# Order of the elements in the PSUM eviction of the gate products (hybrid decoder step, 1 core)

## The chip, the cores and the metric

The kernel runs on one core of one Trainium2 chip. The time is device microseconds of one execution; before the change the median of 3 runs is 2963.49 us (2955.86 to 2965.84).

## The reference, cut to what matters

One inference step of two layers for 512 prompt tokens and 8 sample tokens. Each layer is a token mixer, a layer norm, a PEER block and another layer norm. The change lies in the PEER block. Per token it picks 8 heads x 16 experts out of 16384 and adds up their contributions:

```python
expert = jnp.take_along_axis(cand_idx, pos, axis=-1)
gate = jax.nn.softmax(best, axis=-1)
act = jax.nn.gelu(jnp.einsum('td,thkd->thk', tb, u_tab[expert]).astype(F32))
return jnp.einsum('thk,thkd->td', (gate * act).astype(tb.dtype), v_tab[expert])
```

## The kernel before, in words

The first 384 prompt tokens (three token tiles of 128) are computed densely, over all 16384 experts. An expert has the number i*128 + j; the 128 experts with the same i form a block, and j is the partition. For each block, `u_step` (line 354) multiplies the block's weights with the 384 tokens in 24 matmuls (`pu`, lines 91 to 93: f16 high and low halves) and ScalarE applies the gelu into `act` (line 366). The weights of a block come by DMA into `wst`; ScalarE rounds them to `wh` (line 77) and VectorE makes the rest `wl` (line 86). `wh` and `wl` have two buffers each, and `wst` three. The other 128 prompt tokens and the 8 sample tokens use gathered rows instead (`gather`, line 387; `g_dot`, line 394).

For the dense tokens the kernel needs the gate of every (expert, token) pair, which is zero except for the 128 chosen experts of a token. `gates` (line 514) makes them for 32 tokens at a time, 12 calls per layer. For 8 tokens VectorE builds four one-hot arrays `oh` (lines 530 to 533); TensorE multiplies them per token, two 128x128 matmuls each (lines 537 and 538), into one PSUM bank `pg` that holds four tokens as [token][i]; there are four such banks. ScalarE then copies `pg` into `stage` (line 540, by the helper of line 77), an SBUF tile of [i][32 tokens] per partition j. After eight such copies `stage` goes to DRAM (`GD`, line 544), 2 MB on the queue of ScalarE. `stage` has one buffer, so the first copy of a call waits until the transfer of the call before has landed.

The calls of `u_step` stand between the calls of `gates`: two before the copies of a call and one in its middle (lines 518 and 543). Between the groups of four calls stands the top-k work for the next token tile (`pairs`, line 488, on VectorE). A scheduler fixes the order on each engine at build time; each engine then runs its own queue in that order.

After the gates follows the main phase: `gl<-GD` loads the gates back, VectorE multiplies them with `act` (line 640), and TensorE multiplies the product with the value rows (`yps`, line 654), with the remaining `u_step` calls between. Its buffers `yac`, `row` and others lie where `stage` lay.

Of the kernel before, what the change touches and what calls it, by code (L numbers as in the profile page):

```python
# [70 lines left out]
class Kern:  # L71
# [249 lines left out]
    def peer(self, layer):  # L321
# [51 lines left out]
        def run_u(k):  # L373
            for _ in range(k):
                u_step()
# [99 lines left out]
        with tc.tile_pool(name="gates", bufs=1, reuse_waits="tile") as gp, \  # L475
# [38 lines left out]
            def gates(t, part, us):  # L514

                lt = lts[t]
                stage = gp.tile([P, P, TG], F32, name="stage")
                run_u(us - 1)
                order = self.last_on(S)
                for t4 in range(0, TG, 4):  # L520
                    if t4 % 8 == 0:

                        sl = slice(part * TG + t4, part * TG + t4 + 8)

                        def tok(k):
                            return lt[:, k, sl].rearrange("p (a b) -> p a b", b=2)[:, :, None, :].to_broadcast([P, 4, P, 2])

                        io = self.iota2[:, None].to_broadcast([P, 4, P, 2])
                        oh = gp.tile([P, 4, 4, P, 2], F16, name="oh", bufs=2)
                        V.tensor_tensor(oh[:, 0], io, tok(1), op=OP.is_equal)  # L530
                        V.tensor_tensor(oh[:, 1], io, tok(0), op=OP.is_equal)
                        V.tensor_mul(oh[:, 2], oh[:, 1], tok(2))
                        V.tensor_mul(oh[:, 3], oh[:, 1], tok(3))
                    pg = psum.tile([P, 4, P], F32, name="pg", bufs=4)
                    for k in range(4):
                        q, r = divmod(t4 % 8 + k, 2)
                        T.matmul(pg[:, k], oh[:, 0, q, :, r], oh[:, 2, q, :, r], start=True, stop=False)
                        T.matmul(pg[:, k], oh[:, 0, q, :, r], oh[:, 3, q, :, r], start=False, stop=True)  # L538
                    with self.behind(order):
                        self.copy(stage[:, :, t4:t4 + 4].rearrange("p i t -> p t i"), pg)  # L540
                    order = []
                    if t4 == TG // 2:
                        run_u(1)
                nc.scalar.dma_start(GD[P // TG * t + part], stage)
# [20 lines left out]
            for k in range(12):  # L565
                gates(k // 4, k % 4, self.UG)
                acc[0] += self.GU
                while acc[0] >= 1:
                    g_ustep()
                    acc[0] -= 1  # L570
                if k % 4 == 3 and k < 11:
                    run_u(self.UP)
                    pairs(k // 4 + 1)
                    pairs_t(k // 4 + 1)
# [1176 lines left out]
```

## Time and profile before

| what | value |
|---|---|
| median of 3 runs | 2963.49 us |
| time of the profiled execution | 2954.78 us |
| its span | 2953.1 us |
| granted TensorE clock, mean | 0.989 |
| TensorE busy (PE) | 2824.2 us, 96% |
| VectorE busy (DVE) | 2501.0 us, 85% |
| ScalarE busy (ACT) | 1351.7 us, 46% |
| GpSimd busy (POOL) | 956.7 us, 32% |
| copies `stage<-pg` | 192, 182.7 us in sum |

The 192 copies lie in two stretches, from 598.8 us on in the first layer and up to 2215.3 us in the second. PE stands for matmuls, PEld for the loads of their weights; DVE, ACT and POOL are VectorE, ScalarE and GpSimd. A row of a view gives a line of the program, the engine, the operation, the tile written and the tiles read, and the shape as partitions x elements. Busy shares are averages over stages with different limits, and a matmul's row lasts longer than the step from one matmul to the next.

### The profile page before, as it was taken

The numbers are of one execution on the slowest core, as the hardware profiler recorded it, in microseconds if no ns is written. First come the engines' busy times: TensorE is split into PE (matmuls) and PEld (weight loads), VectorE is DVE, ScalarE is ACT, GpSimd is POOL, SyncE is SP. The second block draws the span as 40 slices with busy tenths as digits, with TensorE's granted clock in tenths as the row PEclk, the third lists the DMA queues.
The fourth block names the chain that finished last, engine by engine and source line by source line (L and its number), as shares of the span: only waits on it lengthen the run. The fifth ranks groups of instructions, "written<-read, shape, count | busy, mean of one in ns | idle before, by whom it ended". The sixth has DMA issues, their size and how long they took to land.

```text
span 2953.1 us, 49153 instructions
## 1 busy us (share of the span) xinstructions
PE 2824.2 (96%) x18198; PEld 1714.9 (58%) x18198; DVE 2501.0 (85%) x5483; ACT 1351.7 (46%) x2127; POOL 956.7 (32%) x702
## 2 busy tenths in 40 slices
PE   8999999899999999999998999989999999999998
PEld 7787686466655555544447658646665555554443
DVE  6755789999878898889985869999988889888998
ACT  4733473266743333333435747236674333333332
POOL 2300151310034554445530014140005455444652
PEclk9999999999999999999999999999999999999999
DMA  4223495975699999999984348686569999999996
GB/s 134 71 83 129 147 330 193 311 253 199 225 380 357 372 362 369 360 324 375 354 289 162 106 144 299 238 296 223 211 252 382 355 374 363 355 347 346 330 368 223
DMA packets 320324, 811.33 MB, mean 275 GB/s; under 512 B 28099, under 2 KB 150411, under 8 KB 316244
## 3 DMA queue, kind: packets, MB, share of 16 engines
q1 hardware_dynamic: 229228, 455.37, 44.7%
q0 software_dynamic: 78336, 285.25, 26.0%
q10 hardware_dynamic: 12520, 67.58, 6.2%
q8 instruction: 142, 2.33, 0.3%
q14 instruction: 98, 0.80, 0.1%
HBM read 707.25 MB, written 99.46 MB: 273 GB/s over the span
## 4 chain that ended last, share of the span: by engine, by line
PE 59%; DMA 13%; DVE 12%; ACT 7%; issue 6%; POOL 3%; ACTq 0%; SPq 0%; POOLq 0%; DVEq 0%
PE yps L654 24%; PE pu L93 7%; PE pu L91 7%; PE pu L92 7%; DMA row<-in_u_rows,elist 3%; DMA gl<-GD 3%; ACT stage L77 2%; POOL row L390 2%; DMA gst<-in_uT 1%; DVE row L397 1%; ACT wh L77 1%; DVE wl L86 1%; PE psg L1034 1%; DMA row<-in_v_rows 1%; PE pg L538 1%
## 5 line engine op out<-in xcount | busy, mean ns | idle before, releaser
L654 PE MATMUL yps<-vv,vw 128*128 128x512 f16 x4536 | 1008.4, 380 | 10.4 <-DVE vv L86 8.4
L654 PEld LDWEIGHTS <-vw 128*128 128x128 f16 x4608 | 450.7, 98 | 546.1 <-issue 19.6
L390 POOL DMA_INDIRECT row<-in_v_rows,elist x272 | 398.1, 1463 | 836.3 <-ACT stage L77 425.0
L93 PE MATMUL pu<-xh,wl 128*128 128x384 f16 x1728 | 565.8, 329 | 28.5 <-DVE wl L86 28.1
L91 PE MATMUL pu<-xh,wh 128*128 128x384 f16 x1728 | 567.5, 328 | 21.7 <-ACT wh L77 21.7
L92 PE MATMUL pu<-xl,wh 128*128 128x384 f16 x1728 | 566.9, 328 | 0.0
L390 POOL DMA_INDIRECT row<-in_u_rows,elist x272 | 385.8, 1418 | 509.5 <-DVE yac L592 129.3
L86 DVE SCALAR_TENSOR_TENSOR wl<-wst,wh 128x1024 f16<-128x1024 f32 x284 | 351.3, 1240 | 165.8 <-ACT wh L77 151.7
L77 ACT ACTIVATE wh<-wst 128x1024 f16<-128x1024 f32 x284 | 299.3, 1054 | 403.5 <-PE pu L92 293.3
L77 ACT ACTIVATE vv<-row 128x1024 f16<-128x1024 f32 x252 | 264.2, 1051 | 369.6 <-PE yps L654 291.7
L91 PEld LDWEIGHTS <-wh 128*128 128x128 f16 x2816 | 279.9, 99 | 166.3 <-ACT wh L77 39.1
L93 PEld LDWEIGHTS <-wl 128*128 128x128 f16 x2816 | 277.5, 99 | 168.5 <-DVE wl L86 38.5
L86 DVE SCALAR_TENSOR_TENSOR vv<-row,vv 128x1024 f16<-128x1024 f32 x252 | 307.7, 1222 | 63.6 <-ACT vv L77 60.2
L92 PEld LDWEIGHTS <-wh 128*128 128x128 f16 x2816 | 277.7, 99 | 132.8 <-issue 5.9
L592 DVE SCALAR_TENSOR_TENSOR yac<-row,wgt,yac 128x1024 f32<-128x1024 f32 x268 | 343.3, 1281 | 8.7 <-DMA row<-in_v_rows,elist 6.7
L397 DVE CUSTOM_DVE_ANT_0 row<-row,xtok 128x1024 f32<-128x1024 f32 x256 | 308.4, 1220 | 20.7 <-DMA row<-in_u_rows,elist 20.5
L77 ACT ACTIVATE vw<-act 128x384 f16<-128x384 f32 x256 | 129.3, 514 | 226.8 <-PE yps L654 191.5
L77 ACT ACTIVATE stage<-pg 128x512 f32<-128x512 f32 x192 | 182.7, 1104 | 71.1 <-DMA GD<-stage 42.9
L366 ACT ACTIVATE act<-pu 128x384 f32<-128x384 f32 x256 | 121.7, 477 | 87.0 <-PE pu L93 86.1
L84 DVE TENSOR_TENSOR vw<-act,vw 128x384 f16<-128x384 f32 x256 | 139.3, 553 | 13.8 <-ACT vw L77 13.4
L640 DVE TENSOR_TENSOR act<-act,gl 128x384 f32<-128x384 f32 x256 | 127.6, 552 | 11.2 <-DMA gl<-GD 9.1
L92 PE MATMUL pq<-xl,wh 128*128 128x264 f16 (+1 forms) x480 | 132.9, 277 | 0.7 <-DVE xl L84 0.7
(502 smaller groups left out, 4138.8 us busy)
## 6 DMA issues: line engine op xcount, KB each, us to landing
row<-in_v_rows SPq DMA_DIRECT2D x256, 512.0 KB
wst<-in_uT SPq DMA_DIRECT2D x216, 512.0 KB
GD<-stage ACTq DMA_DIRECT2D x24, 2048.0 KB
gl<-GD SPq DMA_DIRECT2D x64, 768.0 KB
gst<-in_uT SPq DMA_DIRECT2D x40, 512.0 KB
PW<-gpr SPq DMA_DIRECT2D x40, 512.0 KB
wpr<-PW SPq DMA_DIRECT2D x40, 512.0 KB
wst<-in_wq SPq DMA_DIRECT2D x32, 512.0 KB
```

Of the source, the lines that this page charges most:

```text
L77: self.nc.scalar.activation(out, in_, AF.Copy, scale=scale)
L84: eng.tensor_sub(lo, src, hi)
L86: eng.scalar_tensor_tensor(lo, src, scale, hi, op0=OP.mult, op1=OP.subtract)
L91: mm(out, wh, xh, start=start, stop=False)
L92: mm(out, wh, xl, start=False, stop=False)
L93: mm(out, wl, xh, start=False, stop=stop)
L366: S.activation(t, ps[:, 0:ND], AF.Gelu_apprx_tanh, scale=1.0 / SCW)
L390: G.indirect_dma_start(out=r, out_offset=None, in_=src, in_offset=bass.IndirectOffsetOnAxis(ap=elist[:, k:k + 1], axis=0))
L397: V.tensor_tensor_reduce(u, u, self.xtok[:, 0] if k < P else xrep, 1.0, 0.0, OP.mult, OP.add, hd[:, k:k + 1])
L592: V.scalar_tensor_tensor(dst, vbuf.pop(n), wgt[:, k:k + 1], dst, op0=OP.mult, op1=OP.add)
L640: V.tensor_mul(a6, a6, gl)
L654: T.matmul(yps[t][:, o], w[:, a, c], v[:, b, o], start=x == 0 and k == 0, stop=x == P - 1 and k == 2)
```

## The change

One line. The copy of a PSUM bank of four tokens into `stage` walks through both tiles in another order. Before, it read `pg` from end to end, and wrote each token's 128 values into `stage` with a step of 32 elements (128 bytes). After, it writes for each i four tokens in a row (16 bytes; the next four elements are 128 bytes on), and reads `pg` with a step of 128 elements (512 bytes), four times, then goes on to the next i. What is computed, the number of instructions, and the order on every engine stay the same.

```diff
                     with self.behind(order):
-                        self.copy(stage[:, :, t4:t4 + 4].rearrange("p i t -> p t i"), pg)
+                        self.copy(stage[:, :, t4:t4 + 4], pg.rearrange("p t i -> p i t"))
                     order = []
```

## Rows read from the trace of the kernel before

**Rows 1.** Page, part 1 (busy time) and part 4 (chain, by line).
```profile
PE 2824.2 (96%) x18198; PEld 1714.9 (58%) x18198; DVE 2501.0 (85%) x5483; ACT 1351.7 (46%) x2127; POOL 956.7 (32%) x702
...
PE yps L654 24%; PE pu L93 7%; PE pu L91 7%; PE pu L92 7%; DMA row<-in_u_rows,elist 3%; DMA gl<-GD 3%; ACT stage L77 2%; POOL row L390 2%; DMA gst<-in_uT 1%; DVE row L397 1%; ACT wh L77 1%; DVE wl L86 1%; PE psg L1034 1%; DMA row<-in_v_rows 1%; PE pg L538 1%
```

**Rows 2.** Busy time by stretch, first layer: start:end, length, busy (instructions), granted clock, DMA.
```profile
core 0: us, PE busy (x) PEld busy (x) DVE busy (x) ACT busy (x) POOL busy (x), PEclk, DMA share, GB/s
598.00:690.00 92.00, 86.52 (x688) 56.82 (x686) 88.79 (x219) 61.74 (x78) 5.34 (x4) 1.00 0.66 231
690.00:828.00 138.00, 135.91 (x1165) 92.86 (x1163) 118.88 (x170) 96.67 (x120) 3.40 (x3) 1.00 0.65 235
```

**Rows 3.** ACT, groups by line and form: count | busy us, mean ns | idle before.
```profile
L77 ACT ACTIVATE stage<-pg 128x512 f32<-128x512 f32 x192 | 182.7, 1104 | 71.1 <-DMA GD<-stage 42.9 <-PE pu L92 24.0 <-PE pg L538 4.1
...
L77 ACT ACTIVATE scs<-psc 128x512 f32<-128x512 f32 x32 | 19.0, 595 | 9.0 <-issue 8.3 <-PE psc L445 0.7
...
L77 ACT ACTIVATE ss<-psc 128x8 f32<-128x8 f32 x32 | 5.8, 182 | 0.0
...
L77 ACT ACTIVATE xh<-pst 64x64 f16<-64x64 f32 x2 | 0.4, 218 | 2.0 <-PE pst L1546 2.0
```

**Rows 4.** Waits of PE, 598 to 690 us: us in total, times, longest.
```profile
PE pu L91 <- ACT wh L77: 3.5, 2, 2.1
PE pu L93 <- DVE wl L86: 2.0, 3, 1.1
```

**Rows 5.** Waits of DVE, 598 to 690 us.
```profile
DVE wl L86 <- ACT wh L77: 2.3, 2, 1.9
DVE lt L510 <- ACT lt L77: 0.5, 1, 0.5
```

**Rows 6.** Waits of PE, 690 to 828 us.
```profile
PE pu L91 <- ACT wh L77: 1.3, 4, 0.4
PE pu L93 <- DVE wl L86: 0.8, 1, 0.8
```

**Rows 7.** ACT in order of time, 750 to 778 us: start, length, instruction, idle before.
```profile
752.00 3.73 ACT L77 ACTIVATE stage<-pg 128x512 f32<-128x512 f32 x4 [3.69 <-DMA GD<-stage]
...
756.86 3.77 ACT L77 ACTIVATE stage<-pg 128x512 f32<-128x512 f32 x4
760.65 0.33 ACTq L544 DMA_DIRECT2D GD<-stage  x1
...
767.85 3.77 ACT L77 ACTIVATE stage<-pg 128x512 f32<-128x512 f32 x4 [3.98 <-DMA GD<-stage]
```

**Rows 8.** PE in order of time, 776.9 to 778.6 us.
```profile
777.26 0.33 PE L92 MATMUL pu<-xl,wh 128*128 128x384 f16 x1
777.42 0.33 PE L93 MATMUL pu<-xh,wl 128*128 128x384 f16 x1
...
778.11 0.34 PE L91 MATMUL pu<-xh,wh 128*128 128x384 f16 x1 [0.24 <-ACT wh L77]
...
778.50 0.22 PE L537 MATMUL pg<-oh 128*128 128x128 f16 x1
778.56 0.22 PE L538 MATMUL pg<-oh 128*128 128x128 f16 x1
```

**Rows 9.** Waits of PE, second layer, 1998 to 2082 us.
```profile
PE pu L91 <- ACT wh L77: 3.6, 3, 1.8
PE pu L93 <- DVE wl L86: 2.4, 3, 1.1
```

**Rows 10.** Waits of DVE, second layer, 1998 to 2082 us.
```profile
DVE wl L86 <- ACT wh L77: 2.9, 1, 2.9
```

**Rows 11.** Waits of PE, second layer, 2082 to 2220 us.
```profile
PE pu L91 <- ACT wh L77: 1.1, 3, 0.4
```

**Rows 12.** DVE in order of time, just after the last copy of the first layer.
```profile
835.33 0.75 DVE L590 TENSOR_SCALAR yac<-row,wgt 128x1024 f32<-128x1024 f32 x1 [2.42 <-DMA GD<-stage]
```

## The prediction

> **What bounds the kernel now.** I read the page first, then the stretches with the gate copies, then who waits for whom in them. TensorE is busy 96% of the span, ScalarE, whose copies change, 46%, and in the chain of work that ended last the copies `stage<-pg` hold 2% [rows 1], some 59 us of 2953. So a change to a ScalarE copy counts only where somebody stands still because of it. The copies lie in two stretches of about 230 us, one per layer, and each has two parts [rows 2]. From 598 to 690 us VectorE is busy 88.79 of 92 us: the top-k work paces this part. From 690 to 828 us TensorE is busy 135.91 of 138 us and VectorE 118.88: here TensorE paces. The second layer repeats this from 1998 and 2082 us on.
>
> In the first part TensorE waits 3.5 us for `wh` from ScalarE and 2.0 us for `wl` from VectorE [rows 4]. VectorE itself waits 2.3 + 0.5 us for ScalarE [rows 5]. In the second part TensorE waits 1.3 + 0.8 us [rows 6]. The reason stands in ScalarE's queue [rows 7]: the first copy of a call waits for the transfer of the call before (issued at 760.65, next copy at 767.85), four copies take 3.77 us, and the `wh` of a weight block stands behind them. Everything the copies can give back is in these few waits.
>
> **The price of one copy.** A `stage<-pg` of 512 elements takes 1104 ns, a plain eviction of the same 128x512 f32 `scs<-psc` takes 595 ns [rows 3]. The surplus is 509 ns, 0.99 ns for each element that is written 128 bytes from the one before. After the change the write has runs of 16 bytes, and the read takes on the stride. No eviction of this trace reads 512 elements with a 512-byte step, so I bound it. The nearest row is `xh<-pst` 64x64, which reads PSUM with a step of 16 elements (64 bytes): 218 ns [rows 3]. Between 182 ns for 8 plain elements and 595 ns for 512, 64 plain elements would take 182 + 56 x 0.82 = 228 ns. So the stepped read cost nothing; a surplus of 0.99 ns an element would have made it 291. One end is therefore 595 ns. For the write I allow one surplus for each new run of 16 bytes, 128 x 0.99 = 127 ns, which gives 722 ns. The far end is that the 512-byte step costs in the read what the old step cost in the write: 1104 ns. I take about 600 ns, by the row nearest in kind: that is 0.5 us less, 192 x 0.5 = 97 us less of ScalarE's work in all.
>
> [...]
>
> **What of it lies on the path.** Most of the 97 us is cover: ScalarE waits after a group of copies anyway, 42.9 us for the transfer and 24.0 us for TensorE in sum [rows 3]. By parts:
>
> - *598 to 690 us.* With shorter copies the transfer is issued sooner, the next copies start sooner, and `wh` comes sooner: four copies of 0.5 us are 2.0 us, as long as the longest wait of TensorE (2.1) and of VectorE (1.9) [rows 4, 5]. TensorE's waits sum to 5.5 us, and a little more, since a matmul row lasts 0.33 us while the next starts 0.16 us later, so each wait hides 0.17 us more of lost issue [rows 8]. But VectorE, with no other idle time, cannot move up by more than its own waits for ScalarE, 2.3 + 0.5 = 2.8 us, and TensorE takes `wl` from it. I count 2.8 us.
> - *690 to 828 us.* TensorE's five waits: 2.1 us shown plus 5 x 0.17 = 2.9 us. Each is shorter than the 2.0 us that four copies give, so I count all of it. Check by one period: the calls repeat after 767.85 - 752.00 = 15.85 us [rows 7]. TensorE needs 72 x 0.162 + 64 x 0.057, about 15.3 us (steps between the rows of [rows 8], 0.16 and 0.06). The loop of the one `stage` buffer is now just as long: 7.20 us of transfer and 8.65 us from the first copy to the issue [rows 7]. With 8 copies 0.5 us shorter it takes 11.9 us, and TensorE alone sets the period: 0.5 us per call is there to win, no more.
> - *1998 to 2082 us.* TensorE waits 3.6 + 2.4 us [rows 9], VectorE 2.9 us for ScalarE [rows 10], and 0.5 us for `lt` once more, word for word the second row of [rows 5]: 3.4 us. By the same limit 3.4 us.
> - *2082 to 2220 us.* 1.1 us in three waits [rows 11] and one of 0.8 us, word for word the second row of [rows 6]; with 4 x 0.17, 2.6 us.
> - *Into the main phase.* After the last copies VectorE waits 2.42 us for the transfer before it can write `yac` [rows 12]. The last four copies put that transfer 2.0 us earlier against TensorE. What is late next there is the weight blocks' own chain of loads; I take 0.5 us per layer, from bounds of 0 and 2.0.
>
> Sum: 2.8 + 2.9 + 3.4 + 2.6 + 1.0 = 12.7 us. The main phase starts earlier by it and runs on as before. A copy of 722 ns would give the same in the TensorE-paced parts and about 1 us less in the others. The profiled execution takes 2954.78 us (span 2953.1), and would take 2942; the median shown is 8.7 us above it, 2963.49, and 12.7 us less is about 2951.
>
> **The rivals.**
> 1. *The gain is caught by the engines next in line.* If in the first parts the freed VectorE time is taken up by waits for TensorE or the weight loads, only the TensorE-paced parts give: 2.9 + 2.6 = 5.5 us, time 2958. For it: 88.79 of 92 us busy. Against it: the waits of rows 5 and 10 are for ScalarE alone.
> 2. *The copy does not get faster,* since the stride only moves into PSUM: 0 us, 2963.5. [...]
> 3. *The whole chain share goes.* If the 59 us of copies in the chain [rows 1] shrink by 509/1104, 27 us go: 2936. Against it: where the copies are in the chain, TensorE runs beside them nearly without a gap [rows 2].
> 4. *Slower: the stepped read costs more than the stepped write did.* Then the buffer's loop, already as long as the period, becomes the bound. Every ns over 1104 counts 8 times a call in 24 calls; from 46 ns on, 1150 ns per copy, it is 0.3%. If a read step cost 1.5 times what the write step cost, the copy would take 595 + 764 = 1359 ns, and the time would grow by 255 ns x 8 x 24 = 49 us to 3012. Only a penalty that no row shows at 64 bytes would do this.
>
> **How the numbers follow.** A measurement of this kernel tells about 0.3% from no change, 8.9 us. Forecast 0.60 (8 to 17 us less; in 0.52 of it over 8.9 us); rival 1 0.22; rival 2 0.08; rival 3 0.05; rival 4 0.05. Faster: 0.52 + 0.05 = 0.57. Same: 0.08 + 0.22 + 0.08 = 0.38. Slower 0.05. The range goes from 2938 (just short of rival 3, with the forecast's upper bound of 17 us and the 5 us or so by which runs differ) to 2964 (rival 2 included). The forecast's own range is 2946 to 2956.
>
> **What would show it.** Right: `stage<-pg` at 595 to 722 ns; the period in the second part 15.3 to 15.5 us; TensorE's waits for `wh` and `wl` there near zero; VectorE's waits for ScalarE gone in the first parts; the last copy of the first layer 5 to 6 us earlier, of the second 11 to 12. Wrong: a copy near 1100 ns; or a fast copy with the last copies no earlier, because VectorE or the weight loads keep the pace; or a start of the main phase that loses again what the gates won.

## The result, and the profile after

| | before | after |
|---|---|---|
| median of the runs | 2962.43 us (2953.41 to 2976.45, 20 runs) | 2946.97 us (2939.16 to 2959.06, 20 runs) |
| profiled execution | 2954.78 us, span 2953.1 | 2946.15 us, span 2944.4 |
| ratio of the runs | | 0.9949, 95% interval 0.9937 to 0.9961 |

The change makes the kernel 15 us faster (11.6 to 18.7 by the interval, times 2962). Forecast were 12.7 us less and 2951 us, with a range from 2938 to 2964. The two profiled executions differ by less, 8.6 us, since that of before lies near the low end of its runs.

The page of the changed kernel, part 1 (busy time) and part 4 (chain, by line):

```profile
PE 2826.9 (96%) x18198; PEld 1716.8 (58%) x18198; DVE 2501.1 (85%) x5483; ACT 1275.1 (43%) x2127; POOL 960.2 (33%) x702
...
PE yps L654 25%; PE pu L93 8%; PE pu L91 8%; PE pu L92 8%; DMA gl<-GD 3%; DMA row<-in_u_rows,elist 3%; POOL row L390 1%; DVE row L397 1%; PE psg L1034 1%; DVE wl L86 1%; PE pg L538 1%; PE pg L537 1%; DMA gst<-in_uT 1%; PE pmix L92 1%; PE pmix L93 1%
```

Against [rows 1], ScalarE has 76.6 us less work, and `stage` on line 77 is no longer in the chain, where it had 2%. Nothing else in the first line moved by over 4 us.

ScalarE's groups by line and form, the row that answers to the first of [rows 3]:

```profile
L77 ACT ACTIVATE stage<-pg 128x512 f32<-128x512 f32 x192 | 100.3, 601 | 67.2 <-DMA GD<-stage 37.0 <-PE pg L538 30.2
```

A copy takes 601 ns instead of 1104. The copies give ScalarE back 82.4 us (182.7 - 100.3), and the kernel gains some 15 of them.

The same stretches of the first layer as in [rows 2], up to the same matmuls (597 to 687 and 687 to 821.6 us here), and TensorE's waits in the first one, as in [rows 4]:

```profile
597.00:687.00 90.00, 87.72 (x696) 57.37 (x694) 89.69 (x222) 48.86 (x78) 5.77 (x4) 1.00 0.68 240
687.00:821.60 134.60, 134.60 (x1162) 92.77 (x1160) 117.93 (x168) 71.73 (x119) 3.06 (x3) 1.00 0.68 239
```

```profile
PE pu L93 <- DVE wl L86: 0.8, 1, 0.8
PE pg L538 <- DVE oh L533: 0.6, 2, 0.3
PE pu L91 <- ACT wh L77: 0.5, 1, 0.5
PE pg L537 <- DVE oh L532: 0.2, 1, 0.2
```

VectorE is now busy 89.69 of 90 us in the first stretch and waits for nobody; in [rows 5] it had waited 2.8 us for ScalarE. TensorE's waits there fell from 5.5 us to 2.1, and all but the 0.5 are for VectorE. In the second stretch TensorE is busy without a gap.

ScalarE in order of time there, as in [rows 7]:

```profile
761.44 2.07 ACT L77 ACTIVATE stage<-pg 128x512 f32<-128x512 f32 x4 [1.24 <-DMA GD<-stage]
...
768.11 2.06 ACT L77 ACTIVATE stage<-pg 128x512 f32<-128x512 f32 x4 [2.17 <-PE pg L538]
770.21 0.33 ACTq L544 DMA_DIRECT2D GD<-stage  x1
```

Four copies last 2.07 us instead of 3.77. What counts is the wait in front of the second group: it is now for `pg`, so ScalarE is ahead of TensorE in the middle of a call. In [rows 7] that group followed without idle time: ScalarE was behind.

The gain can be read from the gate matmuls themselves. The first four rows are line 538 in the kernel before: first five calls and last seven calls of layer one, then of layer two (from the first start to the last start). The next four are the changed kernel.

```profile
L538 PE MATMUL pg<-oh x160: 217/218/222, 597.5 to 704.0; 128*128 128x128 f16 x160
L538 PE MATMUL pg<-oh x224: 218/218/221, 712.2 to 820.2; 128*128 128x128 f16 x112
L538 PE MATMUL pg<-oh x160: 218/218/222, 1987.9 to 2096.6; 128*128 128x128 f16 x160
L538 PE MATMUL pg<-oh x224: 217/218/221, 2104.7 to 2212.5; 128*128 128x128 f16 x112
```

```profile
L538 PE MATMUL pg<-oh x160: 217/218/222, 596.8 to 700.6; 128*128 128x128 f16 x160
L538 PE MATMUL pg<-oh x224: 218/218/221, 708.7 to 815.3; 128*128 128x128 f16 x112
L538 PE MATMUL pg<-oh x160: 218/218/222, 1988.9 to 2092.8; 128*128 128x128 f16 x160
L538 PE MATMUL pg<-oh x224: 217/218/221, 2100.9 to 2207.5; 128*128 128x128 f16 x112
```

The first five calls are 2.7 and 4.8 us shorter (106.5 to 103.8, 108.7 to 103.9), the last seven 1.4 and 1.2 (108.0 and 107.8 to 106.6). That is 10 us inside the calls.

Both kernels issue their 18198 matmuls in the same order, so each matmul can be set beside its partner. Just behind the last gate matmul the kernel before still has the last two waits of its second stretch, and the changed kernel has none there. First three matmuls of the kernel before, then the same three of the changed one:

```profile
825.71 0.34 PE L91 MATMUL pu<-xh,wh 128*128 128x384 f16 x1 [0.42 <-ACT wh L77]
825.88 0.33 PE L92 MATMUL pu<-xl,wh 128*128 128x384 f16 x1
826.97 0.34 PE L93 MATMUL pu<-xh,wl 128*128 128x384 f16 x1 [0.76 <-DVE wl L86]
```

```profile
820.22 0.33 PE L91 MATMUL pu<-xh,wh 128*128 128x384 f16 x1
820.39 0.33 PE L92 MATMUL pu<-xl,wh 128*128 128x384 f16 x1
820.55 0.33 PE L93 MATMUL pu<-xh,wl 128*128 128x384 f16 x1
```

From the last gate matmul to the third of these it takes 6.8 us before and 5.3 after, another 1.5 us.

The start of the main phase is the last place where the prediction expected something. VectorE's first `yac` of the changed kernel, the row that answers to [rows 12]; then TensorE's wait for `wl` there, and the busy times and clock of the 3 us behind it:

```profile
829.51 0.75 DVE L590 TENSOR_SCALAR yac<-row,wgt 128x1024 f32<-128x1024 f32 x1 [3.03 <-DMA GD<-stage]
```

```profile
837.41 0.50 PE L93 MATMUL pu<-xh,wl 128*128 128x384 f16 x1 [2.35 <-DVE wl L86]
```

```profile
838.00:841.00 3.00, 3.00 (x11) 1.45 (x10) 3.00 (x4) 0.00 (x0) 1.95 (x2) 0.50 1.03 408
```

The wait of the kernel before at the same place:

```profile
843.24 0.50 PE L93 MATMUL pu<-xh,wl 128*128 128x384 f16 x1 [1.75 <-DVE wl L86]
```

The last copies and their transfer are issued 7.8 us earlier (824.15 before, 816.33 after), but the transfer takes longer, 13.2 us instead of 11.2 until `yac` can start. `yac` and the `wl` behind it come 5.8 us earlier, no more. TensorE, which had come 6.4 us earlier to that point, waits 2.35 us instead of 1.75. After this wait the granted clock was 0.50 in both kernels (in the row above, and from 843.7 to 846 us in the kernel before): 10 matmuls in a row, some 0.5 us long and 0.32 us apart, ran so in the kernel before and 17 after. From the last gate matmul to the first product `yps` it took 32.1 us before and 32.3 after.

### The profile page after: what moved, and what is told of

The parts are those of the page before. It is cut to its first block, busy times and chain, and to the rows that moved or that the text cites. A ratio compares the mean times of both kernels' runs of the same rounds, so it can differ in the third digit from the quotient of the medians.

```text
span 2944.4 us, 49153 instructions
## 1 busy us (share of the span) xinstructions
PE 2826.9 (96%) x18198; PEld 1716.8 (58%) x18198; DVE 2501.1 (85%) x5483; ACT 1275.1 (43%) x2127; POOL 960.2 (33%) x702
## 4 chain that ended last, share of the span: by engine, by line
PE 65%; DMA 13%; DVE 12%; issue 5%; ACT 3%; POOL 2%; ACTq 0%; SPq 0%; DVEq 0%; POOLq 0%
PE yps L654 25%; PE pu L93 8%; PE pu L91 8%; PE pu L92 8%; DMA gl<-GD 3%; DMA row<-in_u_rows,elist 3%; POOL row L390 1%; DVE row L397 1%; PE psg L1034 1%; DVE wl L86 1%; PE pg L538 1%; PE pg L537 1%; DMA gst<-in_uT 1%; PE pmix L92 1%; PE pmix L93 1%
## 5 line engine op out<-in xcount | busy, mean ns | idle before, releaser
L77 ACT ACTIVATE wh<-wst 128x1024 f16<-128x1024 f32 x284 | 299.2, 1054 | 471.2 <-PE pu L92 368.4
L91 PE MATMUL pq<-xh,wh 128*128 128x264 f16 (+1 forms) x480 | 133.1, 277 | 0.0
```

What stands on the lines that cost most here:

```text
L77: self.nc.scalar.activation(out, in_, AF.Copy, scale=scale)
L91: mm(out, wh, xh, start=start, stop=False)
```

## The experiments

In each table and expectation, "the first five calls" runs from the first gate matmul of a layer to the last of its fifth call, and "the last seven calls" from there to the last gate matmul. Times in us, layer one / layer two, from one profile each. "Old" is the copy with the stepped write, "new" the changed one.

| kernel | copies in calls 1 to 4 | in calls 5 to 12 | first five calls | last seven calls | last gate matmul to first `yps` |
|---|---|---|---|---|---|
| before | old | old | 111.4 / 113.5 | 116.2 / 115.9 | 32.1 / 32.2 |
| after | new | new | 108.6 / 108.8 | 114.7 / 114.7 | 32.3 / 30.7 |
| e1 | new | old | 107.9 / 108.8 | 116.3 / 116.0 | 32.8 / 32.0 |
| e12 (e1 again) | new | old | 108.7 / 108.9 | 116.3 / 116.0 | 32.4 / 32.8 |
| e2 | old | new | 112.5 / 115.7 | 114.7 / 114.7 | 32.4 / 31.3 |
| e13 (e2 again) | old | new | 112.0 / 116.1 | 114.7 / 114.7 | 31.2 / 32.4 |
| e8 | old, 53 ns longer | old, 53 ns longer | 113.8 / 113.5 | 117.8 / 117.9 | 33.2 / 34.0 |
| e9 | new, 87 ns longer | new, 87 ns longer | 108.7 / 109.4 | 114.7 / 114.7 | 32.2 / 32.5 |
| e10 | new | new | 108.7 / 109.5 | 114.7 / 114.7 | 32.1 / 31.6 |
| e11 (after again) | new | new | 108.6 / 109.4 | 114.7 / 114.7 | 32.3 / 32.8 |

**Each part alone.** The new copy only in the first four calls of a layer (e1), or only in the other eight (e2); the edit is against the changed kernel:

```diff
-                        self.copy(stage[:, :, t4:t4 + 4], pg.rearrange("p t i -> p i t"))
+                        self.copy(*((stage[:, :, t4:t4 + 4], pg.rearrange("p t i -> p i t")) if t == 0 else (stage[:, :, t4:t4 + 4].rearrange("p i t -> p t i"), pg)))
```

(e2 has `t > 0`.) The theory and the rivals for e1:

> New copy only in the first four calls of each layer (the part that VectorE paces), old copy in the other eight. Theory (each wait behind the copies gives back its own length): the fifth call starts about 3 us earlier in the first layer and 3 to 5 us earlier in the second, measured from the first call of the same layer; from there on the period stays 15.85 us; in all 6 us less than before, ratio 0.998. Rival (VectorE's pace eats what the first part wins): the fifth call no earlier, ratio 1.000.

For e2:

> Old copy in the first four calls, new copy in the other eight (the part that TensorE paces). Theory: the first part as before, then a period of 15.4 us in place of 15.85 us; 5.5 us less from the periods and up to 3.3 us from the two last copies, of which the start of the main phase may take some back; ratio 0.997 to 0.998. Rival (the whole gain of 15 us comes from here): ratio 0.995.

Measured: e1 2953.18 us against 2966.1, ratio 0.996 (0.9938 to 0.9982); e2 2957.36, ratio 0.997 (0.9954 to 0.9985). The ratios (11.9 and 8.9 us) add up to some 21 us, more than the whole, with wide intervals. The table is sharper: each part of a layer gains where its own copies are new, and only there.

Both were run again, with 12 runs each instead of 9:

> The kernel of e1 once more, in more rounds, beside that of e2: what is each part's share of the gain? Theory (what the traces of the gate calls show): in nine profiles so far the first five calls of a layer took 111.4 to 115.7 us with the old copy in the first four of them (mean 113.4) and 107.9 to 109.5 with the new one (mean 108.7), so the new copy there is worth 4.7 us in each layer, 9.4 us: ratio 0.9968. In the profile the first five calls at 107.5 to 109.5 us, the last seven at 116.0 to 116.4. Rival: the ratios of the first timing, 0.996 for this part and 0.997 for the other, are the true ones; then the two parts together give 20 us, more than the whole change, and at least one of them has to fall back.

> The kernel of e2 once more, in more rounds. Theory (the traces of the gate calls): the last seven calls of a layer took 115.9 to 116.3 us with the old copy and 114.7 with the new one in every profile, so the new copy there is worth 1.2 to 1.5 us in each layer, 2.6 us: ratio 0.9991, no change that a measurement can tell. Rival 1 (the first timing, 0.997): the two waits that lie between the last gate copies and the main phase are kept after all, another 1.5 us in each layer, and the main phase gains as well: 0.997 again. In the profile the first five calls at 111 to 116 us, the last seven at 114.7 under both; the stretch from the last gate matmul to the first product of the main phase at 32 us under the theory, 30.5 under the rival.

Measured: e12 2954.87 against 2965.66, ratio 0.9966 (0.9952 to 0.998), 10.1 us; e13 2958.09, ratio 0.9977 (0.9962 to 0.9992), 6.8 us. The layers' rows of line 538, first of e12 and then of e13 (first five and last seven calls of layer one):

```profile
L538 PE MATMUL pg<-oh x160: 217/218/222, 597.7 to 701.5; 128*128 128x128 f16 x160
L538 PE MATMUL pg<-oh x224: 218/218/221, 709.6 to 817.8; 128*128 128x128 f16 x112
```

```profile
L538 PE MATMUL pg<-oh x160: 217/218/222, 596.0 to 703.1; 128*128 128x128 f16 x160
L538 PE MATMUL pg<-oh x224: 218/218/221, 711.2 to 817.8; 128*128 128x128 f16 x112
```

The first five calls took 113.56 us in the mean of the four kernels with old copies there (before, e2, e13, e8) and 108.82 in that of the six with new ones: 4.7 us a layer (3.9 in layer one, 5.6 in layer two), 9.5 in all, as e12's ratio says, where e1's theory had 6. The last seven took 116.1 with the old copies (before, e1, e12) and 114.7 with the new: 1.4 us a layer. For e13 the theory's 0.9991 is just inside the interval; its ratio and that of e2 both say more than the 2.8 us of the trace, and what makes the other 4 us isn't shown. A small piece is the last column: 32.4 us in the mean with old copies in the later calls (e8 left out), 32.0 with new ones, 0.4 us a layer.

With the old copies the first five calls took from 111.4 to 116.1 us, with the new ones from 107.9 to 109.5. Part of what varies is TensorE's granted clock, as one pair of profiles shows. In layer two the kernel before and e2 have the same two waits for `wh` (1.84 and 1.33 us before, 1.82 and 1.33 in e2). Behind the second one, first in the kernel before, where the granted clock stays at 1.00 (2022 to 2028 us), then in e2 with its clock, and VectorE's wait of e2 between 2026 and 2040 us:

```profile
2022.52 0.34 PE L91 MATMUL pu<-xh,wh 128*128 128x384 f16 x1 [1.33 <-ACT wh L77]
2022.69 0.33 PE L92 MATMUL pu<-xl,wh 128*128 128x384 f16 x1
```

```profile
2030.67 0.50 PE L91 MATMUL pu<-xh,wh 128*128 128x384 f16 x1 [1.33 <-ACT wh L77]
2030.97 0.53 PE L92 MATMUL pu<-xl,wh 128*128 128x384 f16 x1
2030.60:2036.40 5.80, 5.72 (x18) 2.69 (x19) 5.05 (x11) 2.24 (x4) 0.00 (x0) 0.50 0.51 172
DVE oh L530 <- PE pg L538: 2.9, 1, 2.9
```

In e2 the granted clock is 0.50 there, and 19 `pu` matmuls follow each other in 0.32 us instead of 0.16, some 3 us in all; VectorE, which paces this part, then waits 2.9 us for TensorE. The eight first parts with old copies have 66 such slow matmuls (none of them in the kernel before), the twelve with new ones 8 (all in e9). At 0.16 us each that is, as an estimate, 1.3 us a layer (0.8 without e8, whose copies are longer) against 0.1. Why the clock is 0.50 behind these waits in one execution and 1.00 in another isn't shown.

**The price of a copy by itself.** Behind the changed kernel's own work, ScalarE and then VectorE copy 512 f32 of a PSUM bank to SBUF, with one side stepped: the read by 1, 2, 4, 16, 64 and 128 elements, then the write by 2, 4, 8, 16 and 32, then writes in runs of 2, 4 and 8 elements 128 bytes apart, then the changed and the old pattern, three copies of each:

```diff
+                for rd in (1, 2, 4, 16, 64, 128):
+                    src = pz.rearrange("p (a b) -> p b a", b=rd) if rd > 1 else pz
...
+                for wr in (2, 4, 8, 16, 32):
+                    dst = sz[:, 0:512 * wr].rearrange("p (a b) -> p a b", b=wr)[:, :, 0]
...
+                for run in (2, 4, 8):
+                    dst = sz[:, 0:512 // run * 32].rearrange("p (a b) -> p a b", b=32)[:, :, 0:run]
```

> The changed kernel with 90 more copies of 512 f32 elements from one PSUM bank to SBUF at its end, on ScalarE and on VectorE, three of each pattern. Theory: on ScalarE a step in the PSUM read costs nothing at any step (2 to 128 elements: about 597 ns), a step in the SBUF write of 16 bytes or more costs the full 0.5 us (4, 8, 16 and 32 elements: about 1100 ns) and a step of 8 bytes or runs of 4 cost nothing. [...] Third: the write price grows with the step from 4 to 32 elements.

Measured by the trace, ns of one copy (the kernel's own time with this appendix, 3025.52 us, is of no use):

| | ScalarE | VectorE |
|---|---|---|
| read step 1, 2, 4, 16, 64, 128 elements, plain write | 597 each | 690 to 692 each |
| write step 2 elements (8 bytes) | 619 | 691 |
| write step 4 (16 bytes) | 1067 | 1054 |
| write step 8 | 1086 | 1072 |
| write step 16, 32 | 1024 | 1011 |
| write in runs of 2, 4, 8 elements | 597 | 691 |
| read by 128, write in runs of 4 (the changed pattern) | 597 | 691 |
| write step 32, token by token (the old pattern) | 1024 | 1011 |

The rows of ScalarE's 18 stepped reads, of four copies across the border between write steps 2 and 4 (min/median/max), and of the three in the old pattern:

```profile
L77 ACT ACTIVATE srz<-prz x18: 597/597/598, 2945.9 to 2956.6; 128x512 f32<-128x512 f32 x18
L77 ACT ACTIVATE srz<-prz x4: 619/619/1067, 2957.2 to 2959.2; 128x512 f32<-128x512 f32 x4
...
L77 ACT ACTIVATE srz<-prz x3: 1024/1025/1025, 2979.7 to 2981.8; 128x512 f32<-128x512 f32 x3
```

The stepped reads from PSUM took as long as the plain copy: 597 ns on ScalarE and 690 to 692 on VectorE at each step. On ScalarE the write cost 0.83 to 0.96 ns more per element (1024 to 1086 less 597, over 512) at steps of 16 to 128 bytes, and next to nothing at a step of 8 bytes (22 ns a copy) or in runs of two (0). So the 595 to 722 ns of the prediction close at the low end.

**Does each ns of the copy count eight times a call?** A copy with a bias takes a little longer; that lengthens the old copy (e8) and the new one (e9) without touching the order. The bias adds -0.5 to every gate in both.

```diff
-                        self.copy(stage[:, :, t4:t4 + 4].rearrange("p i t -> p t i"), pg)
+                        S.activation(stage[:, :, t4:t4 + 4].rearrange("p i t -> p t i"), pg, AF.Identity, bias=self.mhalf[:, 0:1])
```

> The kernel before, each copy of the gate products with a per-partition bias operand (it adds -0.5 to every gate, so the gates are not the reference's), which the kv rows of this trace price at about 93 ns more per instruction: about 1197 ns per copy. Theory (the loop of the one stage buffer is the bound only once its slack is used up, in the last calls of a layer): 0.74 us more per call for about four calls per layer, and 1 to 2 us per layer in the first part; 7 to 10 us more, ratio 1.003. Rival (every ns of a copy counts in every call, as rival 4 of the prediction priced it): 18 us more, ratio 1.006. Third (copies are cover): 1.000.

> The changed kernel with the same bias operand (-0.5 on every gate, so not the reference's gates): about 691 ns per copy in place of 598. Theory (the gain is used up once the waits behind the copies are gone; TensorE and VectorE set the pace): the period stays 15.4 us, the time is that of the changed kernel, ratio to the kernel before 0.995. Rival (the time follows ScalarE's work): 18 us of the work come back, ratio 1.000 or 1.001.

Measured: the old copy took 1157 ns in the mean instead of 1104, the new one 688 instead of 601. e8: 2966.4 us against 2966.16, ratio 0.9999 (0.9985 to 1.0013). e9: 2948.84, ratio 0.9941 (0.992 to 0.9962), as the changed kernel. ScalarE of e8 in order of time, in the TensorE-paced part:

```profile
772.10 3.92 ACT L540 ACTIVATE stage<-pg,mhalf 128x512 f32<-128x512 f32 x4 [4.70 <-DMA GD<-stage]
777.10 3.96 ACT L540 ACTIVATE stage<-pg,mhalf 128x512 f32<-128x512 f32 x4
...
788.30 3.93 ACT L540 ACTIVATE stage<-pg,mhalf 128x512 f32<-128x512 f32 x4 [4.70 <-DMA GD<-stage]
```

The period is 16.20 us here (788.30 - 772.10), against 15.85 in [rows 7]: the loop of the buffer does lengthen with the copy. But it paces only the last calls of a layer. In the calls before, TensorE's own period is longer than the loop: the sixth to ninth take 19.75, 17.8, 15.69 and 15.37 us in the kernel before and in the changed one alike. So in the last seven calls e8 loses 1.6 and 2.0 us (117.8 and 117.9 against 116.2 and 115.9), not the 10 us that the price of the fourth rival gives for 53 ns (53 ns x 192 copies; the expectation's 18 us had counted 93 ns). That price is refuted: the times tell no loss, and the interval ends at 3.9 us. The theory's 7 to 10 us, also for 93 ns, wasn't met either. That 87 ns on the new copy cost nothing agrees with the waits in front of its groups, 1.24 and 2.17 us above.

**A second stage buffer for the old copy.** If the loop of the one buffer paces the last calls, a second buffer takes it away with old copies too. It needs memory: the ring of `act` buffers is cut from 50 to 43, which moves work about, so e4 has the cut alone and e5 the cut and the second buffer.

```diff
-                stage = gp.tile([P, P, TG], F32, name="stage")
+                stage = gp.tile([P, P, TG], F32, name="stage", bufs=2)
...
-            self.RING, self.NSP, self.UG, self.GU, self.ROWS = 50, 32, 3, 3, 9
+            self.RING, self.NSP, self.UG, self.GU, self.ROWS = 43, 32, 3, 3, 9
```

> The kernel before with 43 in place of 50 buffers for act, which frees the room that the next run needs; the partner for that run. The second part of the gates as in the kernel before: period 15.4 us at first, 15.85 us in the last calls.

> The same with two stage buffers and the old, slow copies. Theory (the loop of one buffer, transfer and then copies, holds back wh and with it TensorE): first copies no longer wait for the transfer, period 15.4 us in all calls of the second part, TensorE's waits for wh there below 0.3 us in all; 5 to 12 us less than its partner. Rival (wh stands behind four slow copies whatever the transfer does): the waits and the 15.85 us stay, no difference from its partner.

Measured, one run each: 2966.68 and 2964.52 us, so 2.2 us less where e5's theory had 5 to 12. ScalarE in layer two, first of e4, then of e5:

```profile
2173.39 3.77 ACT L77 ACTIVATE stage<-pg 128x512 f32<-128x512 f32 x4 [4.00 <-PE pu L92]
...
2189.29 3.77 ACT L77 ACTIVATE stage<-pg 128x512 f32<-128x512 f32 x4 [4.01 <-PE pu L92]
```

```profile
2169.65 3.81 ACT L77 ACTIVATE stage<-pg 128x512 f32<-128x512 f32 x4 [2.17 <-PE pg L538]
...
2185.03 3.81 ACT L77 ACTIVATE stage<-pg 128x512 f32<-128x512 f32 x4 [2.17 <-PE pg L538]
```

The copies are as slow in both (3.77 and 3.81 us for four), and the period falls from 15.90 to 15.38, the changed kernel's. So in the last calls it is the loop of one buffer, not the copy as such, that had cost 0.5 us a call. The fifth call ends at the same time in both to 0.1 us (107.4 and 107.5 us after the first gate matmul in layer one, 109.8 and 109.9 in layer two): there the second buffer gives nothing. But this doesn't settle the first part of the kernel before. In the order of e4 the old copies need hardly more there than the new ones elsewhere, and TensorE's longest wait for `wh` is 1.0 us (2.1 in the kernel before), so little is left to win. The copies hold up `wh` behind them in ScalarE's queue [rows 4, 5, 10]; whether by their own length or by their late start, behind the transfer, stays open for the first part. (The name behind e4's waits is the one that came last by the profile; `pu` on line 92 had been done.)

One more thing stands in these two traces. In layer one the cut moved work so that the last calls of e4 take 18 to 20 us, and the second buffer brings the last seven from 129.0 to 117.2 us. With the other stretches from the first gate matmul to the first `yps`, e5 is 18 us shorter in both layers together, yet its time is only 2.2 us less: from the first `yps` of layer one to the gates of layer two it took 1146.0 us instead of 1139.1, and from the first `yps` of layer two to the end 719.7 instead of 710.9. Why isn't shown, from one run each; a gain in the gates is not always kept.

**Where do the waits go that lie behind the last copies?** The first `yac` waits for the last transfer, since it lies where `stage` lay [rows 12]. In e10 the sample tokens' half of `yac` has memory of its own, so that the work on it need not wait:

```diff
+        ysam = lp.tile([P, D], F32, name="ysam")
...
-            dst = yac[:, 0 if k < P else 1]
+            dst = yac[:, 0] if k < P else ysam[:]
...
```

> The changed kernel with the first accumulator of the gathered value rows (the part of yac for the samples) in memory of its own, so that VectorE no longer has to wait for the last transfer out of stage before it; the scheduler orders parts of the program anew. Theory (VectorE's wait for that transfer holds back wl, and so TensorE, at the start of the main phase): from the last gate matmul to the first value matmul 28 to 30 us in place of 32 us; 4 to 8 us less than the changed kernel, ratio to the kernel before 0.992. Rival (the loads and the transfer, not the wait, set the 32 us): 32 us as before, ratio 0.995.

And beside it the changed kernel once more:

> The changed kernel once more, for a second profile and a second ratio. Theory: within a layer, from the first gate matmul to the last one of each call, the same to 1.5 us as in its first profile (223.4 and 223.5 us in place of 227.6 and 229.5 us of the kernel before); the parts that the change does not touch (up to the first gate matmul, and between the first value matmul of layer one and the first gate matmul of layer two) move by up to 10 us from execution to execution. Ratio 0.995 to 0.997. Rival (something outside the gates also became faster): these two parts are shorter than in every profile with the old copy.

Measured: e10 2949.0 against 2958.95, ratio 0.9964 (0.9948 to 0.9981); e11 2951.9, ratio 0.9969 (0.9952 to 0.9987). The two don't differ, and e11's interval overlaps that of the first comparison from 0.9952 to 0.9961, some 12 to 14 us. From the first to the last gate matmul of a layer e11 takes 223.4 and 224.1 us (223.4 and 223.5 in the first profile), as its theory had it, and its parts outside are not shorter than in every profile with old copies, so that rival falls. And from the last gate matmul to the first `yps` it takes 32.1 and 31.6 us in e10, as before. ScalarE and TensorE of e10 just there:

```profile
841.92 1.06 ACT L77 ACTIVATE wh<-wst 128x1024 f16<-128x1024 f32 x1 [2.12 <-DMA wst<-in_uT]
```

```profile
843.05 0.50 PE L93 MATMUL pu<-xh,wl 128*128 128x384 f16 x1 [2.70 <-DVE wl L86]
```

With `yac` out of the way, `wh` stands at the load of the weight block instead. The wait for `yac` was not what held the start of the main phase. (The edit also moved other work a little, so this shows that it isn't enough, not every share.)

**Later steps on the value rows, a miss.** In e6 the changed kernel's steps on gathered value rows come later in the main phase:

```diff
-        pace = [0.0]
+        pace = [-12.0]
```

> The changed kernel with the first steps on the gathered value rows put later (pace starts at -12), so that VectorE's first write to yac, which waits for the last transfer out of stage, stands behind the weight halves and the gate products. Theory on the loss at the start of the main phase (VectorE stands before yac, TensorE waits 2 to 2.5 us for wl behind it and then runs at half clock): the wait of TensorE for wl there falls below 0.5 us, the main phase starts 2 to 4 us earlier in each layer, ratio to the changed kernel 0.998, to the kernel before 0.993. Rival (the loss is the transfers' own time): the main phase starts no earlier.

Measured: 3066.55 us, ratio 1.033 (1.0315 to 1.0345). One number moves the order of the whole main phase, and some 100 us are lost there. Up to the main phase of layer one the run still answers: VectorE doesn't wait before `yac` and TensorE not for `wl`, but TensorE now waits for `wh` (the row below, 816.4 to 849 us), and from the last gate matmul to the first `yps` it takes 32.3 us (32.6 in layer two), as the rival had it.

```profile
PE pu L91 <- ACT wh L77: 4.4, 1, 4.4
```

No kernel that was run is shown to be faster than the changed one.

## Why the prediction was right, step by step

- **The copy: right.** About 600 ns were taken, 601 measured. The row that decided, `xh<-pst` with its 218 ns, had a step of 64 bytes only; in e7 the read took 597 ns on ScalarE at each step up to 512 bytes, and 690 to 692 on VectorE. The allowance for the write, one surplus for each new run of 16 bytes, wasn't needed: in e7 ScalarE's writes in runs of 2, 4 and 8 f32 took 597 ns, those with a step of 8 bytes 619, and only those with a step of 16 bytes or more 1024 to 1086.
- **598 to 690 us, 2.8 us: right for this pair of profiles, in part by luck** (111.4 to 108.6 us). The reason was right: VectorE's waits for ScalarE are gone and it has no idle time left. But VectorE itself moved up by 3.5 us from before the gates to `lt`, and by 4.0 in layer two; against the first gate matmul it stood 0.7 us later than in the kernel before in layer one and 0.8 earlier in layer two. Over all profiles layer one gained 3.9 us.
- **1998 to 2082 us, 3.4 us: too small.** 4.8 us were won (113.5 to 108.8), of which 0.8 is that other start of VectorE; over all profiles 5.6 in layer two. The step that failed is "VectorE cannot move up by more than its own waits for ScalarE". Its premise, that VectorE has no other idle time, holds in the profile shown of before, which has no slow `pu` matmul in its first parts. Other executions with the old copies have stretches there with slow matmuls (5.8 us at a granted clock of 0.50, behind a wait for `wh`, in e2), and VectorE then waits for TensorE (2.9 us in e2); by the estimate above this makes some 0.7 to 1.2 of the 4.7 us a layer. The rest of the excess over 3.1 us, the mean of the two terms, is not accounted for.
- **690 to 828 and 2082 to 2220 us, 2.9 and 2.6 us: right, with their mechanism.** Counted from the first gate matmul, TensorE of the changed kernel is 2.8 us ahead at the end of the first part and 5.7 ahead at the `wl` of 826.97 us, so 3.0 us were won between; in layer two 4.8 and 7.4, so 2.7. Over the profiles 1.4 us of it lie within the last seven calls and 1.5 just behind them. The period is TensorE's own, 15.37 us (forecast 15.3 to 15.5), and e5 shows that the loop of one buffer had set the 15.85, in the last three calls of a layer only.
- **The start of the main phase, 1.0 us: wrong, in sign too.** From that `wl` matmul to the first `yps` it took 25.6 us in the mean with old copies in the later calls (before, e1, e12) and 26.7 with new ones (after, e2, e13, e9, e11): 1.1 us a layer are lost, where 0.5 were to be won (e8, with longer copies, and e10, whose matmuls have another order here, are left out). In the first profile of the changed kernel it is 1.8 us in layer one and nothing in layer two. The last transfer of layer one was issued 7.8 us earlier (forecast for the last copy: 5 to 6; 0.7 of it lay ahead of the first gate, and the last copies themselves end sooner). But it took 2.0 us longer, `wl` came later against TensorE, and 17 matmuls instead of 10 ran at a granted clock of 0.50. So the prediction's own sign of being wrong, "a start of the main phase that loses again what the gates won", came in part. "The weight blocks' own chain of loads" was named as what is late next, and e10 and e6 agree: without the wait for `yac` it is `wh` that comes late (in e10 it waits 2.12 us for the load of `wst`, in e6 TensorE waits 4.4 us for it).
- **The sum.** By the means of the profiles the first parts gave 9.5 us instead of 6.2, the second parts 5.8 instead of 5.5, and the start of the main phase -2.2 instead of +1.0: 13.1 us, beside 12.7 forecast. The total is right because two errors of opposite sign nearly cancel, and that is luck. The other stretches are not in this sum.
- **The rivals.** The first (only the TensorE-paced parts) falls: e1 and e12 gain 10 to 12 us without them. The second (copy not faster) falls with 601 ns. The third (the whole chain share, 2936) is too large: the copies left the chain, but TensorE's matmuls took their place in it. The fourth never came to be tried in its condition; its price, every ns eight times in 24 calls, was wrong, as e8 shows: near the border only the last calls feel it.
- **The last copy of layer two** was to come 11 to 12 us earlier. It came 7.4 us earlier (2215.3 to 2207.9 for the start of the last copy). The gates of both layers had won 10 us by then, but the stretches outside moved. In the ten profiles of the table the time up to the first gate matmul runs from 591.1 to 602.3 us, and that from the first `yps` of layer one to the gates of layer two from 1130.8 to 1137.3, so this sign was no good test. The latter took 1132.2 us in the mean with old copies in the first calls and 1135.0 with new ones: part of the gain may be lost there, which these profiles can't decide.

## What to carry to other kernels

When an eviction must transpose, try the step on the PSUM side and keep at least two f32 (here four, 16 bytes) together on the SBUF side: this took the copy from 1104 to 601 ns, and by itself (e7) ScalarE's copy took 597 ns with any of the stepped reads and with writes in runs of 2, 4 or 8 f32, 128 bytes apart, against 1024 in the old pattern. Cost such a gain by the waits of the engine that paces each stretch, not by the copies' busy time (82 us less work on ScalarE, some 15 us less time), and look at each call by itself: a buffer's loop may pace three calls of twelve. A wait can cost more than its length: here a granted clock of 0.50 followed a wait of 1.33 us in e2 and one of 1.00 followed the same wait in the kernel before, and that profile, from which the cap was drawn, had no slow matmuls there. And a gain in one stage can be lost in part at the start of the next (here 1.1 us a layer), where in layer one the last transfer took 2.0 us longer.

## What was not expected of the hardware

- In e7 a stepped read of PSUM took no longer than the plain copy on ScalarE and on VectorE, at each step tried from 2 to 128 f32 (597 and 690 to 692 ns for 512 elements).
- In e7 the price of a stepped write to SBUF was a jump, not a slope: 619 ns at 8 bytes, 1067 at 16, 1086 at 32, 1024 at 64 and 128 on ScalarE, against 597 plain. VectorE paid nothing at 8 bytes (691) and took 1011 to 1072 from 16 on, against 691.
- The old pattern took 1024 ns alone (e7) and 1104 in the mean beside the kernel's other work, while the changed one took 597 and 601. So the old copy took 8% more in that company, the changed one under 1%. What the old one meets there wasn't tried.
- A bias of one value per partition cost 87 ns on the fast copy (601 to 688, e9) but 53 on the slow one (1104 to 1157, e8).
- Behind the same two waits (1.8 and 1.33 us) TensorE's granted clock stayed at 1.00 in the kernel before and was 0.50 for 5.8 us in e2.
